# Later stores of split weights, a one-operation final norm for the last two expert pairs, and one branch around both overflow loops in a decoder block on one core

## The chip, the core and the metric

The kernel runs on one core of a Trainium2 chip. The metric is the device time of one execution in microseconds (us). The core has a matrix engine (TensorE, PE in the profile, with its weight loads PEld), a vector engine (VectorE, DVE), a scalar engine (ScalarE, ACT), a general engine (GpSimd, POOL) and SyncE (SP), which here only issues transfers. Each issues its instructions in order and waits for others by semaphores. A transfer (DMA) is issued by an engine's queue, and all transfers share 16 DMA engines. An instruction that waits in such a queue holds back what stands behind it.

## What is computed

The reference is one block of a hybrid decoder on 2048 tokens of width 1024, in float32. Cut to what matters here:

```
h = rmsnorm(x, norm1_g);  proj = h @ w_in            # q, k, v, r, a_low, u_pool and two gates
o = (head_rmsnorm(gla_mix(q, k, v, log_a)) * silu(r)) @ w_gla_branch
p = pool_mix(u_pool) @ w_pool_branch
x = x + (sigmoid(gate_gla) * o + sigmoid(gate_pool) * p) @ w_out
h2 = rmsnorm(x, norm2_g)
x = x + hier_moe(h2, ...)       # a group of 8 experts, 2 of them for each token, 32 in all
return rmsnorm(x, norm_f_g)
```

## The kernel before, in words

**Mixer.** Everything ahead of the experts is done in four blocks of 512 tokens (`block`, b = 0 to 3; the first ends near 250 us, the second near 575). A product is made in float16 with each operand split in a high half (hi) and what that leaves (lo). A 128 x 1024 piece of a weight is loaded as float32 by `stage` (L161). `halves` makes hi with an ACT operation (L177) and lo with a DVE operation (L178). Both lie in one buffer of the pool `wp`, which has 13 buffers (`NW`) for float32 pieces, split pieces and reloads alike. Since all blocks use the same weights, `halves` also stores the split piece to a DRAM tensor `wkeep` (L181), for some kinds of weight in block 0 and for the others in block 1 (`KEEP`); later blocks load it from there (`weight`, L170) and split nothing. In L161, L170 and L181, as in the transposing transfers of activations (L261 in `turn`, L686 in `turned`) and the loads of x (L275), the issuer is the queue of SP. So a store that waits for its lo half holds back what stands behind it there.

```
self.nc.sync.dma_start(f, self.A[mat][i])                                  # L161, in stage
nc.scalar.activation(w[:, 0, c:], f[:, c:], AF.Copy, scale=WSC)            # L177, in halves
nc.vector.scalar_tensor_tensor(w[:, 1, c:], f[:, c:], WSC, w[:, 0, c:], op0=OP.mult, op1=OP.subtract)
getattr(nc, self.KQ).dma_start(self.C[n][:, :, c:], w[:, :, c:])           # L181, KQ = 'sync'
```

A scheduler sets the order of the instructions on each engine in the mixer, working from the program's order and its own estimates; so a change in one place moves others. The matmuls of this part that are spoken of below: L339 (projections), L757 and L774 (the branches and the output product), L725 (folded weights), L522 (parts of the linear attention), L796 (the router's logits, which read the second norm's rows turned by the transfers of L261).

**Experts.** 16 pairs of experts follow (`moe`). For each, a plan of letters gives the order in which the steps are written: S splits weights, U and A are the up products and the activation, X, R and B fetch rows, D adds a product to a row tile and F (`finish`) applies the final norm to it and scatters it to the output. A pair has three row tiles: two of 128 rows x 1024 (i = 0, 1; PE line L1322, DVE line L1325) and one in which two halves of 64 rows stand side by side as 128 x 512 (i = 2; L1334, L1337). A row of a token that takes part in two pairs must only be normed the second time; the flags `l` and `nl` of a row say which. If a pair takes more rows than its tiles hold, `overflow` does the rest, and then no row is normed in `finish` but all at the end.

**The norm in `finish`.** `rstd` squares and sums a tile on ACT (L1365), joins the sums on DVE (L1367 to L1370) and takes the power on POOL (L1371). Then DVE multiplies by the flag (L1344), ACT makes a row factor gf * r + nl (L1346, or twice L1350 for halves of 64 rows) and DVE multiplies the tile by it (L1351). `scatter` (L1284) sends the rows from the queue of POOL. The g2 of the second norm has a copy, `g2q`, scaled by 32 (the root of 1024), which one form of the norm reads (`normed`, L232).

**The end.** `overflow` loads a count from memory on every engine (L1380), runs a loop so many times (L1382), loads a second count (L1438) and runs a second loop (L1439). With the inputs given both counts are zero. L1529 is the program's last line: what it shows is the end of the program on every engine.

Of the kernel before, what the change touches and what calls it, by code (L numbers as in the profile page):

```python
# [7 lines left out]
F32 = mybir.dt.float32  # L8
F16 = mybir.dt.float16
# [7 lines left out]
D = 1024  # L17
# [19 lines left out]
class Mixer:  # L37
# [10 lines left out]
    def pools(self):  # L48
# [14 lines left out]

        self.C, self.kept = tc.dram_tile([16 + 40 + 24, 128, 2, 1024], F16, name="wkeep"), {}
# [24 lines left out]
    def consts2(self):  # L89
# [22 lines left out]
        self.g2q = self.cx.tile([128, D], F32, name="g2q")  # L112
        V.tensor_scalar(self.g2q, self.g2, float(D) ** 0.5, None, op0=OP.mult)
# [45 lines left out]
    def stage(self, mat, i):  # L159
        f = self.wp.tile([128, 1024], F32, name="w", bufs=self.NW)  # L160
        self.nc.sync.dma_start(f, self.A[mat][i])  # L161
        return f

    def weight(self, mat, i, f=None, c=0):
# [5 lines left out]
        nc.sync.dma_start(w[:, :, c:], self.C[self.kept[mat, i]][:, :, c:])  # L170
        return w

    def halves(self, f, key, c=0):
# [42 lines left out]
    def normed(self, x, g, store=None, quick=False, new=None):  # L216

        nc = self.nc
        if quick:
# [11 lines left out]
            for y, n in zip(ys, q):  # L231
                nc.vector.scalar_tensor_tensor(y, x[:, n], r[:, 0:1], self.g2q[:, n], op0=OP.mult, op1=OP.mult)  # L232
# [569 lines left out]
    def block(self, b, tail):  # L802

        last = b + 1 == self.NB
        self.blk = b
        self.hT, self.L7, self.L7c = self.hTn, self.sevens(self.Hn, self.HSn), self.sevens_c(self.Hn, self.HSn)
# [56 lines left out]
        if last:  # L863
            self.xo = {t: self.x_load(b, t) for t in range(TT)}
# [206 lines left out]
    def spill(self):  # L1071
# [31 lines left out]
        V.tensor_scalar(none[:, 0:1], none[:, 0:1], 0.5, None, op0=OP.is_lt)  # L1103
        for _, _, l, _ in self.tab:
# [26 lines left out]
    def moe(self):  # L1131
# [18 lines left out]
        with tc.manual_schedule(engines={getattr(E, e) for e in self.MANUAL}) if self.MANUAL else ExitStack():  # L1150
            for P in range(self.NP + 1):
                for c in (self.PLAN if P else self.PLAN.replace("U0 A0 U1 A1", "V0 V1 W0 A0 W1 A1")).split():
# [186 lines left out]
    def finish(self, s, i):  # L1339

        nc = self.nc
        x, o, _, l, nl = s["X"][i]
        y, r = self.rstd(x)
# [7 lines left out]
        nc.vector.tensor_tensor(y, x, y, op=OP.mult)  # L1351
        t = self.scatter(y, o).ins
# [21 lines left out]
    def overflow(self):  # L1374
# [7 lines left out]
        with tc.For_i(0, n):  # L1382
            T = lambda name, sh, dt=F32: mp.tile([128] + sh, dt, name="o" + name)
            le = T("le", [32])
            V.tensor_scalar(le, self.ct, self.it, None, op0=OP.is_le)
            e = T("e", [1])
            V.tensor_reduce(e, le, axis=AX.X, op=OP.add)
            ei = T("ei", [1], I32)
            V.tensor_copy(ei, e)
            V.tensor_scalar(le, self.i32, e, None, op0=OP.is_equal)  # L1390
            st = T("st", [32])
            V.tensor_tensor(st, self.ct, self.nt, op=OP.subtract)
            V.tensor_tensor(st, st, le, op=OP.mult)
            base = T("base", [1])
            V.tensor_reduce(base, st, axis=AX.X, op=OP.add)
            V.tensor_tensor(base, self.it, base, op=OP.subtract)
            V.tensor_tensor(st, self.capE, le, op=OP.mult)
            cap = T("capt", [1])
            V.tensor_reduce(cap, st, axis=AX.X, op=OP.add)
            V.scalar_tensor_tensor(base, base, 128.0, cap, op0=OP.mult, op1=OP.add)  # L1400
            rel, oth = T("rel", [nt * 2]), T("oth", [nt * 2])
            V.tensor_scalar(oth, self.ex.rearrange("p t k -> p (t k)"), e, OOB, op0=OP.not_equal, op1=OP.mult)
            V.tensor_scalar(rel, self.rk.rearrange("p t k -> p (t k)"), base, None, op0=OP.subtract)
            V.tensor_tensor(rel, rel, oth, op=OP.add)
            io = T("io", [128])
# [127 lines left out]
```

## Time and profile before

| | us |
|---|---|
| runs: 1673.47, 1674.84, 1676.40; median | 1674.84 |
| the profiled execution's own time | 1676.06 |
| its span, first to last instruction | 1674.3 |
| PE busy | 1530.3 (91%) |
| DVE busy | 1074.3 (64%) |
| ACT busy | 686.0 (41%) |
| POOL busy | 607.7 (36%) |
| mean granted clock of PE | 0.96 of full speed |

The profile is one execution. Its time is 1.8 us above its span and 1.2 us above the median of the runs. Busy times are shares of the whole span; where the engine that sets the pace changes from stage to stage, the tables by stretch tell more than these.

### The profile page before, as it was taken

Reading aid. Unit: us, or ns where it says so; the run is one execution under the profiler, and the core shown is the slowest. Engines: PE = TensorE matmul, PEld = TensorE weight load, DVE = VectorE, ACT = ScalarE, POOL = GpSimd, SP = SyncE. Lnnn points to the kernel's source line nnn. Section 1 sums busy time; section 2 is a strip of 40 time slices with the busy share of each in tenths; the row PEclk is TensorE's granted clock in tenths of the full one; section 3 lists DMA queues with packets and bytes.
Section 4 is the critical chain, followed back from the end, with each engine's and each line's share of the span. In section 5 each row is a group of like instructions: output and inputs, shape, how many; then the busy total and the mean of one; then the engine's idle time right before and its main releaser. Section 6 shows DMA issues by size and latency. Waiting matters only on the chain.

```text
span 1674.3 us, 27694 instructions
## 1 busy us (share of the span) xinstructions
PE 1530.3 (91%) x10587; PEld 914.6 (55%) x10587; DVE 1074.3 (64%) x1898; ACT 686.0 (41%) x1056; POOL 607.7 (36%) x543
## 2 busy tenths in 40 slices
PE   5898978987999898999989999996799999999994
PEld 3364333435744343764434674443668787777773
DVE  8669685589954543772624674337577777777762
ACT  5623453453223352122423021113356665666661
POOL 1356382356523401342322241121343444444431
PEclk9999999989999999999989999998799999999997
DMA  7434659797775989565878756759599999999941
GB/s 267 133 117 141 232 189 249 230 293 234 231 259 164 250 287 286 182 194 179 231 192 246 245 160 201 204 159 315 187 313 332 336 328 341 333 325 326 330 164 43
DMA packets 244808, 394.65 MB, mean 236 GB/s; under 512 B 154507, under 2 KB 157963, under 8 KB 244672
## 3 DMA queue, kind: packets, MB, share of 16 engines
q1 hardware_dynamic: 222144, 324.50, 62.5%
q0 software_dynamic: 22528, 68.35, 11.5%
q8 instruction: 84, 1.38, 0.3%
q14 instruction: 52, 0.43, 0.1%
HBM read 294.03 MB, written 75.50 MB: 221 GB/s over the span
## 4 chain that ended last, share of the span: by engine, by line
PE 66%; DVE 11%; DMA 7%; issue 6%; POOL 4%; SPq 3%; ACT 2%; POOLq 0%; DVEq 0%; ACTq 0%
PE acc L1297 14%; PE aux L339 8%; PE acc L774 8%; PE acc L339 8%; PE acc L1322 7%; PE acc L522 6%; PE acc L757 6%; DMA w<-in_wv_dram 4%; PE acc L1334 3%; DVE w L178 3%; DMA bt<-bt 2%; SPq L261 2%; PE auxh L1241 2%; PE acc L591 1%; POOL w L398 1%
## 5 line engine op out<-in xcount | busy, mean ns | idle before, releaser
L1297 PE MATMUL acc<-xT,mwh 128*128 128x184 f16 (+2 forms) x3264 | 249.8, 239 | 0.0
L1297 PEld LDWEIGHTS <-mwh 128*128 128x128 f16 x3264 | 244.6, 98 | 7.6 <-issue 7.6
L178 DVE SCALAR_TENSOR_TENSOR w<-w 128x1024 f16<-128x1024 f32 x106 | 144.2, 1369 | 88.5 <-ACT w L177 88.2
L774 PE MATMUL acc<-w,bt 128*128 128x512 f16 x768 | 174.4, 389 | 16.1 <-DMA bt<-bt 12.9
L339 PEld LDWEIGHTS <-hS 128*128 128x128 f16 x1056 | 104.5, 100 | 133.4 <-issue 18.0
L757 PE MATMUL acc<-w,bt 128*128 128x512 f16 x768 | 169.0, 381 | 7.1 <-ACT w L177 7.1
L177 ACT ACTIVATE w<-w 128x1024 f16<-128x1024 f32 x106 | 108.0, 1028 | 151.8 <-DMA w<-in_wv_dram 75.2
L1203 DVE SCALAR_TENSOR_TENSOR mwh<-mst,mwh 128x1024 f16<-128x1024 f32 x128 | 153.4, 1219 | 23.6 <-ACT mwh L1202 23.4
L1202 ACT ACTIVATE mwh<-mst 128x1024 f16<-128x1024 f32 x128 | 128.7, 1049 | 60.7 <-PE acc L1297 59.8
L774 PEld LDWEIGHTS <-bt 128*128 128x128 f16 x768 | 76.0, 100 | 113.2 <-issue 14.5
L339 PE MATMUL aux<-w,hS 128*128 128x512 f16 x528 | 131.6, 398 | 4.5 <-DVE w L178 2.5
L339 PEld LDWEIGHTS <-hT 128*128 128x128 f16 x792 | 77.2, 98 | 100.9 <-issue 11.1
L522 PEld LDWEIGHTS <-w 128*128 128x128 f16 x1176 | 114.3, 100 | 32.4 <-issue 10.5
L757 PEld LDWEIGHTS <-bt 128*128 128x128 f16 x768 | 75.3, 98 | 99.9 <-issue 10.9
L339 PE MATMUL acc<-w,hS 128*128 128x512 f16 x528 | 123.1, 382 | 0.0
L1322 PE MATMUL acc<-msd,sg 128*128 128x512 f32 x256 | 115.7, 605 | 0.0
L762 POOL TENSOR_TENSOR et<-et 128x512 f32<-128x512 f32 x32 | 40.5, 1269 | 174.9 <-DVE et L760 174.9
L684 ACT ACTIVATE bt<-et 128x512 f16<-128x512 f32 x48 | 30.2, 628 | 174.4 <-POOL et L762 100.6
L348 DVE SCALAR_TENSOR_TENSOR et<-aux,et 128x512 f32<-128x512 f32 x99 | 65.8, 683 | 53.5 <-PE aux L339 53.5
L339 PE MATMUL aux<-w,hT 128*128 128x512 f16 x396 | 91.8, 379 | 5.7 <-DVE w L178 3.3
L760 DVE SCALAR_TENSOR_TENSOR et<-acc,et 128x512 f32<-128x512 f32 x64 | 43.3, 689 | 82.4 <-PE acc L757 82.4
L339 PE MATMUL acc<-w,hT 128*128 128x512 f16 x396 | 92.3, 379 | 0.9 <-DVE w L178 0.9
(293 smaller groups left out, 2493.8 us busy)
## 6 DMA issues: line engine op xcount, KB each, us to landing
w<-wkeep SPq DMA_DIRECT2D x172, 512.0 KB, 4.7
mst<-in_we_dram SPq DMA_DIRECT2D x128, 512.0 KB, 6.0
wkeep<-w SPq DMA_DIRECT2D x70, 512.0 KB, 3.3
msd<-in_we_dram SPq DMA_DIRECT2D x64, 512.0 KB, 7.1
w<-in_wv_dram SPq DMA_DIRECT2D x60, 512.0 KB, 4.9
x<-in_x_dram SPq DMA_DIRECT2D x32, 512.0 KB, 5.5
w<-in_wm_dram SPq DMA_DIRECT2D x16, 512.0 KB, 6.1
out_dram<-x POOLq DMA_DIRECT2D x16, 512.0 KB, 5.8
```

The source lines that it names most:

```text
L177: nc.scalar.activation(w[:, 0, c:], f[:, c:], AF.Copy, scale=WSC)
L178: nc.vector.scalar_tensor_tensor(w[:, 1, c:], f[:, c:], WSC, w[:, 0, c:], op0=OP.mult, op1=OP.subtract)
L339: nc.tensor.matmul(p, L[name](i, c, k), w[k // 2][:, a, (k % 2) * 512:(k % 2 + 1) * 512], start=k == 0 and m == 0, stop=k == 3 and m == 2)
L348: nc.vector.scalar_tensor_tensor(o[i], ps[i], DSC, x[i], op0=OP.mult, op1=OP.add)
L522: nc.tensor.matmul(ps[:, :h], w[:, i, k * 128:(k + 1) * 128], L[name](c, k), start=k == 0 and m == 0, stop=k == 3 and m == 2)
L757: nc.tensor.matmul(ps, lhs, w[k // 2][:, a, (k % 2) * 512:(k % 2 + 1) * 512], start=k == 0 and i == 0, stop=k == 3 and i == 2)
L774: nc.tensor.matmul(ps, self.mT[t][k // 4][:, 4 * c + k % 4], w[hf][k // 2][:, a, (k % 2) * 512:(k % 2 + 1) * 512], start=k == 0 and i == 0 ...
L1202: nc.scalar.activation(w[:, 0], f, AF.Copy, scale=WSC)
L1203: nc.vector.scalar_tensor_tensor(w[:, 1], f, WSC, w[:, 0], op0=OP.mult, op1=OP.subtract)
L1297: nc.tensor.matmul(ps[:, c * CAP + lo:c * CAP + hi], self.part(W[o], col, 128, a), xT[:, b, k, lo:hi], start=k == 0 and i == 0, stop=k == ...
L1322: nc.tensor.matmul(ps, s["ac"][i][:, f, :128], self.part(s["W"][3 * i + 2], f * D + hf * 512, 512), start=f == 0, stop=f == 1)
L1334: nc.tensor.matmul(ps[hf * 64:(hf + 1) * 64], s["ac"][h][:, f, CAP - 64:], self.part(s["W"][3 * h + 2], f * D + hf * 512, 512), start=q == ...
```

## The change

1. `halves` no longer issues its store. It appends it to a list, `self.stores`, with the number of weight loads issued so far. After each weight load (`stage` or a reload in `weight`) `loaded` issues those stores that are two or more loads old, each with a note to the scheduler that it comes after that load. A list that is not empty is emptied at the start of each block (`flush`).
2. `g2q` is gone. In the last block `g2` is scaled in place, and the norm reads it.
3. Ahead of the experts, `spill` makes a flag `ln`, two small factors `lq` and a copy `gl` of gf for the case that no tile overflowed, with three small DVE operations and one ACT operation.
4. `finish` of pairs 14 and 15 no longer looks at a row's flags. For a 128 x 1024 tile ACT squares two halves into two sums; DVE adds them with the norm's epsilon, POOL takes the power, DVE adjusts it, and one DVE operation multiplies the tile by the row's factor and `gl`. A 64-row tile takes the old `rstd` and two such operations.
5. In the last pair the plan has the 64-row tile first: D2 F2 D0 F0 D1 F1 in place of D0 F0 D1 F1 D2 F2.
6. Both loops of `overflow` stand within one branch on the first count.

```diff
-        self.nc.sync.dma_start(f, self.A[mat][i])
+        self.loaded(self.nc.sync.dma_start(f, self.A[mat][i]).ins)
         return f
+    AHEAD = 2
+    def loaded(self, ins):
+        self.nload += 1
+        while self.stores and self.stores[0][0] + self.AHEAD <= self.nload:
+            with self.tc.issue_after(ins):
+                self.store1()
+    def store1(self):
+        _, n, w, c = self.stores.pop(0)
+        getattr(self.nc, self.KQ).dma_start(self.C[n][:, :, c:], w[:, :, c:])
...
-            getattr(nc, self.KQ).dma_start(self.C[n][:, :, c:], w[:, :, c:])
+            self.stores.append((self.nload, n, w, c))
...
-        V.tensor_scalar(self.g2q, self.g2, float(D) ** 0.5, None, op0=OP.mult)
...
+        V.tensor_copy(self.ln, none[:, 0:1])
+        V.tensor_scalar(self.lq[:, 0:1], none[:, 0:1], float(D) ** 0.5, None, op0=OP.mult)
+        V.tensor_scalar(self.lq[:, 1:2], none[:, 0:1], -1.0, 1.0, op0=OP.mult, op1=OP.add)
+        nc.scalar.activation(self.gl, self.gf, AF.Identity, bias=self.lq[:, 1:2], scale=self.ln[:, 0:1])
...
+                if P == self.NP - 1:
+                    plan = plan.replace("D0 F0 D1 F1 D2 F2", "D2 F2 D0 F0 D1 F1")
...
+                for h in range(2):
+                    c = slice(h * 512, h * 512 + 512)
+                    nc.scalar.activation(y[:, c], x[:, c], AF.Square, accum_out=ss[:, h:h + 1])
+                nc.vector.tensor_scalar(r, ss[:, 0:1], ss[:, 1:2], D * EPS, op0=OP.add, op1=OP.add)
+                nc.gpsimd.tensor_tensor(r, r, self.mhalf[:, 0:1], op=OP.pow)
+                nc.vector.tensor_scalar(r, r, self.lq[:, 0:1], self.lq[:, 1:2], op0=OP.mult, op1=OP.add)
+                nc.vector.scalar_tensor_tensor(y, x, r, self.gl, op0=OP.mult, op1=OP.mult)
...
-        with tc.For_i(0, n):
+        with tc.If(n > 0):
+            with tc.For_i(0, n):
```

The change moves instructions in the whole mixer. Three places matter below. In the rows a number behind a name tells buffers apart; numbers and lines differ between the two programs for the same step (L161 and L160 load a weight, L181 and L174 store a split one, L261 and L277 turn rows, L275 and L291 load x).

**The queue of SP in block 1, where rows are turned for the first logits** (bt_2649 and bt_2650 before, bt_2647 and bt_2648 now). Before:

```order
L161 DMA w_2831<-in_wv_dram 128x1024
L181 DMA wkeep_79<-w_2793 128x2048
L181 DMA wkeep_79<-w_2797 128x2048
L161 DMA w_2833<-in_wv_dram 128x1024
L275 DMA x_4541<-in_x_dram 128x1024
L181 DMA wkeep_79<-w_2837 128x2048
L181 DMA wkeep_79<-w_2841 128x2048
L181 DMA wkeep_79<-w_2906 128x2048
L261 DMA_TRANSPOSE bt_2649<-bt_2575 128x8x128
L261 DMA_TRANSPOSE bt_2650<-bt_2576 128x8x128
```

The same place in the changed program:

```order
L160 DMA w_2827<-in_wv_dram 128x1024
L291 DMA x_4539<-in_x_dram 128x1024
L160 DMA w_2829<-in_wv_dram 128x1024
L174 DMA wkeep_79<-w_2791 128x2048
L174 DMA wkeep_79<-w_2794 128x2048
L277 DMA_TRANSPOSE bt_2647<-bt_2573 128x8x128
L277 DMA_TRANSPOSE bt_2648<-bt_2574 128x8x128
L291 DMA x_4584<-in_x_dram 128x1024
L160 DMA w_3040<-in_wv_dram 128x1024
L160 DMA w_3042<-in_wv_dram 128x1024
L174 DMA wkeep_79<-w_2835 128x2048
L174 DMA wkeep_79<-w_2838 128x2048
```

Three stores (w_2837, w_2841, w_2906) that stood ahead of the two transposes stand behind them, and the load of x stands ahead of the last weight load.

**The queue of SP between block 0 and block 1, where the rows of block 1 are turned** (hT, hS) and weights of block 0's output product are loaded. Before:

```order
L261 DMA_TRANSPOSE hT_2114<-et_2187 128x8x128
L161 DMA w_2249<-in_wv_dram 128x1024
L261 DMA_TRANSPOSE hS_2115<-et_2208 128x8x128
L261 DMA_TRANSPOSE hS_2115<-et_2209 128x8x128
L261 DMA_TRANSPOSE hS_2115<-et_2212 128x8x128
L261 DMA_TRANSPOSE hS_2115<-et_2213 128x8x128
L161 DMA w_2369<-in_wv_dram 128x1024
L275 DMA x_2389<-in_x_dram 128x1024
L275 DMA x_2417<-in_x_dram 128x1024
```

Now:

```order
L277 DMA_TRANSPOSE hT_2108<-et_2183 128x8x128
L277 DMA_TRANSPOSE hS_2109<-et_2204 128x8x128
L160 DMA w_2245<-in_wv_dram 128x1024
L174 DMA wkeep_79<-w_2140 128x2048
L174 DMA wkeep_79<-w_2143 128x2048
L277 DMA_TRANSPOSE hS_2109<-et_2205 128x8x128
L277 DMA_TRANSPOSE hS_2109<-et_2208 128x8x128
L277 DMA_TRANSPOSE hS_2109<-et_2209 128x8x128
L291 DMA x_2387<-in_x_dram 128x1024
L291 DMA x_2415<-in_x_dram 128x1024
L160 DMA w_2367<-in_wv_dram 128x1024
```

The load of w_2249 (now w_2245) has one transpose more ahead of it, and that of w_2369 (now w_2367) two stores and two loads of x more.

**DVE at the end of the last pair** (mx_ tiles are the three row tiles, y the normed rows). Before:

```order
L1337 SCALAR_TENSOR_TENSOR mx_10479<-acc,twr,mx_10479 128x512
L1344 TENSOR_TENSOR frs<-frs,tlm 128x1
L1367 COPY frs<-fss 64x1
L1368 COPY frs<-fss 64x1
L1369 TENSOR_TENSOR fss<-fss,frs 128x1
L1370 TENSOR_SCALAR frs<-fss 128x1
L1351 TENSOR_TENSOR y<-mx_10478,y 128x1024
L1344 TENSOR_TENSOR frs<-frs,tlr 128x1
L1351 TENSOR_TENSOR y<-mx_10479,y 128x512
```

Now:

```order
L1356 SCALAR_TENSOR_TENSOR mx_10477<-acc,twm,mx_10477 128x512
L1394 SCALAR_TENSOR_TENSOR y<-mx_10478,frs,gl 64x512 x2
L1387 TENSOR_SCALAR frs<-frs,slq 128x1
L1385 TENSOR_SCALAR frs<-fs_17137 128x1
L1388 SCALAR_TENSOR_TENSOR y<-mx_10476,frs,gl 128x1024
L1387 TENSOR_SCALAR frs<-frs,slq 128x1
L1388 SCALAR_TENSOR_TENSOR y<-mx_10477,frs,gl 128x1024
```

The operation after the last product (L1337 before, L1356 now) is followed by one that finishes the 64-row tile, and the last operation makes a whole 128-row tile.

## Rows read from the trace of the kernel before

**Rows 1.** The page: share of the chain that ended last, by engine.

```profile
PE 66%; DVE 11%; DMA 7%; issue 6%; POOL 4%; SPq 3%; ACT 2%; POOLq 0%; DVEq 0%; ACTq 0%
```

**Rows 2.** Stretches of 20 us: busy PE, PEld, DVE, ACT, POOL; granted clock; DMA.

```profile
260.00:280.00 20.00, 13.64 (x57) 5.80 (x56) 8.71 (x10) 4.01 (x5) 5.99 (x4) 0.83 1.03 238
...
340.00:360.00 20.00, 15.86 (x88) 7.03 (x87) 18.88 (x20) 13.22 (x19) 10.81 (x9) 0.89 0.90 271
360.00:380.00 20.00, 15.61 (x75) 6.25 (x73) 16.12 (x19) 7.27 (x8) 8.16 (x8) 0.76 1.10 311
...
400.00:420.00 20.00, 13.25 (x104) 10.65 (x104) 20.00 (x45) 4.26 (x7) 13.51 (x10) 0.93 0.49 172
...
sum 340.00, PE 291.98 PEld 154.52 DVE 264.72 ACT 143.81 POOL 179.00; mean PE 17.18 PEld 9.09 DVE 15.57 ACT 8.46 POOL 10.53
```

**Rows 3.** Waits of SP's queue, whole span: total us, times, longest.

```profile
SPq L181 <- DVE w L178: 115.2, 39, 9.2
```

**Rows 4.** Waits of PE, 100 to 430 us: total, times, longest.

```profile
PE aux L796 <- DMA bt<-bt: 7.9, 3, 3.7
PE acc L757 <- ACT w L177: 7.1, 2, 6.4
...
PE aux L725 <- DMA w<-in_wv_dram: 4.5, 2, 3.0
```

**Rows 5.** Waits of SP's queue, 340 to 360 us.

```profile
SPq L181 <- DVE rms L211: 5.4, 1, 5.4
```

**Rows 6.** PE in order of time, 345 to 375 us: start, us, what, idle before.

```profile
344.75 7.07 PE L339 MATMUL acc<-w,hS 128*128 128x512 f16 x32
354.29 0.19 PE L796 MATMUL aux<-wrh,bt 128*128 128x36 f16 x1 [2.47 <-DMA bt<-bt]
...
357.29 4.43 PE L339 MATMUL aux<-w,hS 128*128 128x512 f16 x10
...
370.69 0.21 PE L796 MATMUL aux<-wrh,bt 128*128 128x36 f16 x1 [3.73 <-DMA bt<-bt]
```

**Rows 7.** ACT in order of time, 255 to 300 us.

```profile
280.15 1.06 ACT L177 ACTIVATE w<-w 128x1024 f16<-128x1024 f32 x1 [5.89 <-DMA w<-in_wv_dram]
286.83 1.06 ACT L177 ACTIVATE w<-w 128x1024 f16<-128x1024 f32 x1 [5.62 <-DMA w<-in_wv_dram]
```

**Rows 8.** PE in order of time, 235 to 300 us.

```profile
274.32 6.77 PE L757 MATMUL acc<-w,bt 128*128 128x512 f16 x24 [6.36 <-ACT w L177]
```

**Rows 9.** DVE in order of time, 10 to 40 us.

```profile
20.43 0.69 DVE L113 TENSOR_SCALAR g2q<-g2r 128x1024 f32<-128x1024 f32 x1
```

**Rows 10.** The stretch of the experts, in the columns of rows 2.

```profile
1240.00:1640.00 400.00, 400.00 (x3793) 304.46 (x3791) 295.47 (x481) 249.09 (x330) 164.56 (x162) 1.00 0.88 308
```

**Rows 11.** ACT in order of time, 1185 to 1215 us.

```profile
1203.06 2.00 ACT L1202 ACTIVATE mwh<-mst 128x1024 f16<-128x1024 f32 x2 [13.14 <-PE acc L1297]
```

**Rows 12.** The chain that ended last, in order of time: start, us, what.

```profile
1649.32 3.61 PE acc L1334 x16
```

**Rows 13.** DVE and POOL in order of time, from 1651 us.

```profile
1652.95 0.75 DVE L1337 SCALAR_TENSOR_TENSOR mx<-acc,twr,mx 128x512 f32<-128x512 f32 x1 [0.99 <-PE acc L1334]
...
1655.03 0.15 DVE L1370 TENSOR_SCALAR frs<-fss 128x1 f32<-128x1 f32 x1
1655.66 1.23 DVE L1351 TENSOR_TENSOR y<-mx,y 128x1024 f32<-128x1024 f32 x1 [0.48 <-ACT y L1346]
...
1658.72 0.69 DVE L1351 TENSOR_TENSOR y<-mx,y 128x512 f32<-128x512 f32 x1 [1.76 <-ACTq L1382]
...
1659.68 0.99 POOL L1284 DMA_INDIRECT out_dram<-y,tih  x1 [1.48 <-DVE y L1351]
```

**Rows 14.** Lines L1382, L1439, L1529: ns min/median/max, first and last start.

```profile
L1382 POOLq INC_SWDGE_SEM  x1: 1832/1832/1832, 1661.2 to 1661.2; - x1
...
L1439 POOLq COMPARE_BRANCH  x3: 33/33/39, 1665.2 to 1666.5; - x3
...
L1529 POOLq DRAIN  x3: 40/109/6772, 1666.7 to 1674.0; - x3
```

More of the change, by code (lines that the diff above doesn't have):

```diff
@@ L62, in pools @@
         self.H = tc.dram_tile([self.NTOK, 2, D], F16, name="h2d")
+        self.stores, self.nload = [], 0
         self.C, self.kept = tc.dram_tile([16 + 40 + 24, 128, 2, 1024], F16, name="wkeep"), {}
@@ L160, in stage, with flush @@
         f = self.wp.tile([128, 1024], F32, name="w", bufs=self.NW)
-        self.nc.sync.dma_start(f, self.A[mat][i])
+        self.loaded(self.nc.sync.dma_start(f, self.A[mat][i]).ins)
         return f
+    AHEAD = 2
[7 more added lines that the diff above has]
+        getattr(self.nc, self.KQ).dma_start(self.C[n][:, :, c:], w[:, :, c:])
+    def flush(self):
+        while self.stores:
+            self.store1()
     def weight(self, mat, i, f=None, c=0):
@@ L231, in normed @@
             for y, n in zip(ys, q):
-                nc.vector.scalar_tensor_tensor(y, x[:, n], r[:, 0:1], self.g2q[:, n], op0=OP.mult, op1=OP.mult)
+                nc.vector.scalar_tensor_tensor(y, x[:, n], r[:, 0:1], g[:, n], op0=OP.mult, op1=OP.mult)
             hi = [nc.scalar.activation(hh[0][:, n], y, AF.Copy).ins for y, n in zip(ys, q)]
@@ L863, in block @@
         if last:
+            nc = self.nc
+            nc.vector.tensor_scalar(self.g2, self.g2, float(D) ** 0.5, None, op0=OP.mult)
             self.xo = {t: self.x_load(b, t) for t in range(TT)}
@@ L1151, in moe @@
             for P in range(self.NP + 1):
-                for c in (self.PLAN if P else self.PLAN.replace("U0 A0 U1 A1", "V0 V1 W0 A0 W1 A1")).split():
+                plan = self.PLAN
+                if P == 0:
+                    plan = plan.replace("U0 A0 U1 A1", "V0 V1 W0 A0 W1 A1")
+                if P == self.NP - 1:
+                    plan = plan.replace("D0 F0 D1 F1 D2 F2", "D2 F2 D0 F0 D1 F1")
+                for c in plan.split():
                     f, d = {"U": (self.mo_up, 0), "V": (lambda s, h: self.mo_up(s, h, 0, 128), 0),
@@ L1339, in finish @@
     def finish(self, s, i):
-        nc = self.nc
+        nc, mp = self.nc, self.mp
         x, o, _, l, nl = s["X"][i]
+        if s["P"] >= 14:
+            n = x.shape[1]
+            if n == D:
+                ss = mp.tile([128, 2], F32, name="fs2", bufs=2)
+                r = mp.tile([128, 1], F32, name="frs", bufs=3)
+                y = mp.tile([128, D], F32, name="y", bufs=3)
+                for h in range(2):
[5 more added lines that the diff above has]
+                nc.vector.scalar_tensor_tensor(y, x, r, self.gl, op0=OP.mult, op1=OP.mult)
+            else:
+                y, r = self.rstd(x)
+                nc.vector.tensor_scalar(r, r, self.ln[:, 0:1], self.lq[:, 1:2], op0=OP.mult, op1=OP.add)
+                for h in range(2):
+                    p = slice(h * 64, h * 64 + 64)
+                    nc.vector.scalar_tensor_tensor(y[p], x[p], r[p], self.gl[p, h * 512:(h + 1) * 512], op0=OP.mult, op1=OP.mult)
+            return self.put(s, i, y, o)
         y, r = self.rstd(x)
@@ L1351, in finish, with put @@
         nc.vector.tensor_tensor(y, x, y, op=OP.mult)
+        self.put(s, i, y, o)
+    def put(self, s, i, y, o):
         t = self.scatter(y, o).ins
```

132 lines of the change are left out of this document (67 added, 65 removed).

## The prediction

> **What bounds the kernel now.** I began with the chain that ended last. PE holds 66% of it, then come DVE with 11%, transfers with 7% and the queue of SP with 3% [rows 1]. So PE is the pace, and a gain has to come from where PE stands idle. The table by stretches says where that is. From 1240 to 1640 us PE is busy 400.00 of 400.00 us [rows 10]: in the experts nothing done beside PE can pay. From 100 to 440 us PE is busy 291.98 of 340 us, so 48.0 us are idle [rows 2]. These are block 0 and the first half of block 1, where the weights are split and stored. After the last matmul there is a tail without PE.
>
> Of the 48 us I read who was waited for. Three waits of the logits (L796) for turned rows cost 7.9 us, two of L757 for a hi half 7.1 us, two of L725 for a weight load 4.5 us [rows 4]. In SP's queue the stores (L181) wait 115.2 us in 39 waits for DVE's lo halves [rows 3], and whatever stands behind a waiting store waits too. That is the thing the change attacks. But DVE is itself busy 18.88 of 20 us at 340 to 360 and 20.00 of 20 us at 400 to 420 [rows 2]: there, work that arrives earlier still has to go through DVE.
>
> **The change, part by part.** All of it is a sum of us against the profiled execution; minus is a gain.
>
> *Stores, logits of block 1: -4.* The first logits matmul starts at 354.29 after 2.47 us of waiting for its turned rows, the third wait is 3.73 us [rows 6], and so the second is 7.9 - 2.47 - 3.73 = 1.7 us. In the old order three stores stand ahead of the transposes; one of these waits 5.4 us [rows 5]. In the new order the three stand behind. The two transposes can then go some 5 us or more earlier, which covers the first two waits (4.2 us). The third stays, since five stores stand ahead of its transposes now. Idling also lowers the clock: 32 matmuls took 7.07 us (221 ns each) ahead of the waits, 10 took 4.43 us (443 ns each) behind [rows 6], the two levels 2.4 and 1.2 GHz. The granted clock was 0.89 and 0.76 in the stretches from 340 to 380, worth (0.11 + 0.24) x 20 = 7.0 us of full speed [rows 2], half of it, 3.5 us, behind the first two waits. So at most 4.2 + 3.5 = 7.7 us are to be had. What holds against it is DVE: from 340 to 380 it is idle only 1.1 + 3.9 = 5.0 us, and from 400 on not at all [rows 2], so PE cannot come out further ahead than that. Between 0 and 7.7 I take 4.
>
> *Stores, everywhere else: -1.* The waits of L757 and L725 sum to 11.6 us [rows 4]. The order moves some of their loads ahead of a store, but most of the loads that are late have ten transposes ahead, or stand where DVE is full. Bounds: 0 and -11.6. I take -1, near the DVE row.
>
> *Two loads that come later: +1.5.* Between blocks 0 and 1 the chain is load, hi half, matmul: L757 waits 6.36 us for a hi half [rows 8], and the hi halves at 280.15 and 286.83 follow waits of 5.89 and 5.62 us for their loads [rows 7]. In the new order one of these loads has one transpose more ahead of it, the other two stores and two x loads more, with the transfers busy all the time (share 1.03 at 260 to 280 [rows 2]). PE had no slack there: 274.32 + 6.77 = 281.1 [rows 8] is about where the next hi half was ready. A transpose is bounded by the 2.47 us that PE waited for one pair [rows 6]. Bounds: 0, if the loads were waiting for buffers anyway, and +9.8, a second wait such as the 6.36 us with its clock loss (0.17 x 20 = 3.4 us [rows 2]). I take 1.5, between half a pair of transposes and a whole one.
>
> *g2q: -0.6.* One operation of 0.69 us [rows 9] leaves the start, where DVE works back to back; scaling g2 in the last block costs the same where DVE has room. Bounds -0.7 and 0.
>
> *gl, lq, ln, pair 14: 0.* `gl` is one ACT operation on a tile of 128 x 1024, an estimated 1.2 us by DVE's 1.23 us for that shape [rows 13]; it falls into 13.14 us in which ACT is idle [rows 11]. Pair 14's `finish` runs beside a PE that is 100% busy [rows 10]. If that cover were gone, this would be some 1.2 us more.
>
> *Tail of pair 15: -1.3.* Before, the last matmul ends at 1649.32 + 3.61 = 1652.93 [rows 12] and the last scatter begins at 1659.68 [rows 13], 6.75 us later: product added on DVE, square on ACT, power on POOL, row factor on ACT, product on DVE, one after the other and twice. Now DVE's queue sets the end. Behind the last matmul it does L1356 (0.75, as L1337), two 64-row products (2 x 0.69), three small ones (3 x 0.15) and two of 128 rows (2 x 1.23) [rows 13]: 0.75 + 1.38 + 0.45 + 2.46 = 5.04 us. The chain through ACT and POOL for the last tile runs beside that and is shorter. With some 0.4 us for semaphores the last scatter begins at 5.4, so 1.3 us are gained. That scatter has 128 rows instead of 64 halves, and lands later, but behind it stand 13 us in which nothing waits for it but SP. Bounds -0.5 and -1.7.
>
> *The branch: -3.5.* After the last scatter comes an increment on POOL, 1661.2 + 1.83 = 1663.0; then the second count and the second loop's branches until 1666.5; then a DRAIN on POOL of 6.77 us from 1666.7, and the span ends at 1674.3 [rows 14]. With the branch only the increment stays, so DRAIN can begin at about 1663.2: 1666.7 - 1663.2 = 3.5 us earlier. Bounds: -3.7, all between, and 0. Here a rule speaks against: in the second loop's three branches on POOL, 33 to 39 ns each within 1.3 us [rows 14], I see no stall. The Trainium skill (Runtime: NRT & Kernel Launch, Instruction fetch mechanics) says that a taken branch to a target outside the instructions already fetched waits for them to be fetched. The new branch jumps over both bodies and has no hint ahead of it in the order. By that rule the term would shrink towards 0; by the rows it is -3.5.
>
> Sum: -4 - 1 + 1.5 - 0.6 - 1.3 - 3.5 = **-8.9 us**. From the profiled execution's 1676.06 that gives 1667.2; that execution was 1.2 us above the median of the runs, 1674.84, and from there it gives 1665.9. I forecast **1666.0 us**.
>
> **Rivals.**
>
> *A. DVE binds the mixer, and the stores change nothing there.* For: the 20.00 of 20 us [rows 2]. Against: the logits' waits are for transposes, not for DVE [rows 4]. Then only -0.6, -1.3, -3.5 and +1.5 stay: 1674.84 - 3.9 = 1670.9. The Trainium skill (Perfetto Trace Analysis, Identifying the Most-Contended Engine) says to work first on the engine with the highest occupancy; by that rule moving stores in a queue, with DVE's work as it was, would give this time.
>
> *B. The branch gives nothing,* because DRAIN lasts the longer, waiting for something that ends when it did, or the jump costs what it saves. For: only one DRAIN is seen, and its 6.77 us are not explained [rows 14]. Then 1665.9 + 3.5 = 1669.4.
>
> *C. Slower: a weight load that PE needs comes so late between blocks 0 and 1 that PE stalls once more as at 268 us.* Place and price: 6.36 us [rows 8] and 3.4 us of clock, 9.8 in all, with no gain from the stores. 1674.84 - 5.4 + 9.8 = 1679.2. For: the two x loads now ahead, and the full transfers (1.03 [rows 2]). It decides once the loss is over 5.4 + 3.35 = 8.75 us.
>
> *D. The change doesn't do what it says:* two loads later is often still ahead of the lo half, and the store waits in the queue all the same, with others behind it. Then the mixer keeps its time and the end gains 4.8: 1670.0. For: the third transposes still have stores ahead. Against: the old waits are up to 9.2 us [rows 3], about what two loads take.
>
> **How the numbers follow.** Chances: forecast 0.54, A 0.16, B 0.10, C 0.12, D 0.08. A measurement of this kernel tells about 0.2% from no change, 3.35 us, so "faster" is under 1671.5 and "slower" over 1678.2. The forecast, with terms between their bounds, gives 0.50 of faster and 0.04 of same; A at 1670.9 lies near the line, 0.09 and 0.06 and 0.01 of slower; B 0.08 and 0.02; D 0.06 and 0.02; C 0.10 of slower and 0.02 of same. Sums: 0.73, 0.16, 0.11. The range reaches up past A, B and D to 1675, and leaves out C. Down it takes 7.7 for the logits, 4 for the rest, no late load, and the end's bounds: 1674.84 - 7.7 - 4 - 0.7 - 1.7 - 3.7 = 1657.0.
>
> **What would show it.** Right: the first two logits of block 1 start with no wait, the granted clock from 350 to 365 us is 1.00, SP's stores wait far less than 115 us; the last scatter begins some 5.4 us after the last matmul; POOL's DRAIN begins within 0.5 us of the increment's end and lasts 6.8 us. Wrong: PE's idle time from 100 to 440 us still near 48 us, with DVE in place of transfers as what it waits for (A); a longer DRAIN (B); a new wait of PE for a hi half at 270 to 300 us with half clock behind it (C); long waits of the store line in SP's queue with loads behind them (D).

## The result, and the profile after

The changed kernel takes 1699.07 us (median of 4 runs, 1696.45 to 1702.27) beside 1675.62 for the kernel before; the ratio is 1.0144 with a 95% interval of 1.0121 to 1.0168, so it is **slower by some 24 us**, clear of the noise. I had forecast 1666.0, faster. The profiled execution took 1701.07 us with a span of 1699.3, 25.0 more than the span of before.

To find where the time went I took the nth matmul of PE in either trace and subtracted its start before from its start after. Both have 10587 of them; where their order differs, the difference is only roughly that of one piece of work. (How far two executions in the same order drift apart is told in the last section.) It is 2.8 us at 149 us, 5.2 at 282, 12.4 at 297, 13.4 at 388 and 20.7 from 451 us on, all in the stretch where weights are split and stored. It is 22.7 from about 670 us to the end of the mixer, 26.6 in the experts, and the last matmul ends 27.1 us later (1680.02 against 1652.93). The end gives 2.1 us back, so the span is 25.0 longer.

The windows view of the changed kernel, in the columns of rows 2, shows the stretch; its last row ends at the matmul that stands at 469.3 us in the kernel before:

```profile
100.00:440.00 340.00, 284.29 (x1528) 146.85 (x1527) 248.39 (x335) 142.27 (x211) 177.32 (x110) 0.93 0.70 212
100.00:490.00 390.00, 328.15 (x1843) 179.24 (x1842) 291.12 (x429) 154.48 (x250) 201.62 (x130) 0.93 0.70 212
```

In 340 us PE did less than before (284.29 us busy against 291.98 [rows 2]). The same view of the kernel before, up to the same matmul:

```profile
100.00:469.30 369.30, 321.28 (x1844) 176.03 (x1843) 291.13 (x428) 151.61 (x248) 195.22 (x129) 0.95 0.72 224
```

So for the same matmuls PE needs 20.7 us more: idle time went from 369.3 - 321.28 = 48.0 to 390 - 328.15 = 61.9 us (13.9 more), and busy time rose by 6.9 us, at a granted clock of 0.93 in place of 0.95. DVE's busy time is the same to the hundredth (291.12 and 291.13 us).

What PE waits for, 100 to 440 us of the changed kernel (five of the rows; total us, times, longest):

```profile
PE acc L773 <- ACT w L193: 9.0, 3, 3.7
PE aux L355 <- DVE w L194: 7.4, 4, 2.5
PE acc L790 <- ACT w L193: 6.1, 1, 6.1
PE aux L1002 <- DVE rt32b L999: 4.0, 1, 4.0
PE aux L812 <- DMA bt<-bt: 3.9, 3, 2.1
```

The logits (L812, before L796) do wait less, 3.9 us for 7.9 [rows 4]. Up to the same matmul, all waits for transfers fell from 12.4 to 8.3 us. In their place, those for hi halves (L193) rose from 11.9 to 20.1, and the routing (L1002 and, behind 440 us, L1059), for which PE did not wait before, costs 10.0; those for lo halves (L194) rose from 11.6 to 13.4. What SP's queue waits for, 100 to 480 us, in the changed kernel:

```profile
SPq L174 <- DVE w L194: 58.3, 18, 9.1
SPq L702 <- POOL bt L701: 43.0, 9, 16.5
```

and the row of the stores before, in the same stretch (115.2 in the whole span [rows 3]):

```profile
SPq L181 <- DVE w L178: 93.5, 31, 9.2
```

Summed over all releasers, the stores' waits fell from 171.3 to 84.2 us, those of the transposes rose from 52.9 to 97.7, of the weight loads (L160) from 18.6 to 51.6. The sum over the queue is 257.0 before and 254.7 after. **The queue waits as long as it did; only what it waits in front of has changed.** A queue that either issues or waits can hardly do otherwise in a stretch of fixed length, so this sum alone doesn't show that a shorter wait of the stores is worth nothing. But the queue didn't get through more either: it issued 166 transfers in these 380 us, before 175.

### The profile page after: what moved, and what is told of

Same layout as the page of the kernel before. It is cut to its first block, busy times and chain, and to the rows that moved or that the text cites. A ratio compares the mean times of both kernels' runs of the same rounds, so it can differ in the third digit from the quotient of the medians.

```text
span 1699.3 us, 27530 instructions
## 1 busy us (share of the span) xinstructions
PE 1539.2 (91%) x10587; PEld 917.6 (54%) x10587; DVE 1078.4 (63%) x1903; ACT 682.1 (40%) x1057; POOL 614.8 (36%) x543
## 5 line engine op out<-in xcount | busy, mean ns | idle before, releaser
L194 DVE SCALAR_TENSOR_TENSOR w<-w 128x1024 f16<-128x1024 f32 x106 | 147.2, 1399 | 103.9 <-ACT w L193 103.8
L193 ACT ACTIVATE w<-w 128x1024 f16<-128x1024 f32 x106 | 107.6, 1028 | 154.6 <-DMA w<-in_wv_dram 72.4
```

## The experiments

In the first batch I split the change in parts, with one theory being that the postponed stores cost all of it, and two ways for that: they spoil the order of the work, or the buffers of the weights come free later, so that one buffer more gives the time back.

**e1_stores_at_once**: the change, but each store is issued at once.

```diff
-            self.stores.append((self.nload, n, w, c))
+            getattr(nc, self.KQ).dma_start(self.C[n][:, :, c:], w[:, :, c:])
```

> The changed kernel, with each store issued where it was before (in halves, at once); all other parts of the change stay. Theory H (held buffers): a store that waits for two more loads keeps its buffer of the 13 in use, later weight loads wait for a buffer, PE starves; then nearly all of the mixer's loss is gone, PE's idle time from 100 to 440 us is again near 48 us, and the time is about 1675.6 - 3.2 (branch) + 1.1 (longer end of the last pair) = 1673.5 us, give or take 3. Theory S (reshuffle): any edit makes the scheduler order blocks 0 and 1 anew, by 10 us and more either way, and the stores are not special; then the time lies anywhere from 1665 to 1700 and the mixer differs from before by several us even without the postponed stores. Theory R (the other parts, g2q and gl among them, cost the time): it stays near 1699.

Measured: 1668.28 us, ratio 0.998 (0.9964 to 0.9996), that is -3.3 us. From 451 to 570 us its matmuls stand 0.3 us ahead of those of before, where the change's stood 20.7 us behind.

**e2_stores_only**: the kernel before with `stores`, `loaded`, `store1` and `flush` alone, as in the diff above.

> The kernel before, with the postponed stores as its only edit (list, two loads, emptied at the start of a block). Theory H: the mixer loses some 20 us as in the changed kernel, the end is unchanged: about 1698 us, SP's loads wait 40 us or more for buffers between 100 and 480 us (47 us in the changed kernel, 11 us before). Theory S: a time that differs from the sum of parts by several us, as the scheduler orders it differently again. Theory R: about 1675.

Measured: 1696.02 us, ratio 1.0162 (1.0136 to 1.0187), +27 us. With e1 this closes the sum: 1.0162 x 0.998 = 1.0142, against 1.0144 for the whole. The stores are the whole loss; all else gains 3.3 us.

**e3_branch_only**: the kernel before with `with tc.If(n > 0):` around the two loops.

> The kernel before, with the one branch around both overflow loops as its only edit. From the changed kernel's trace the stretch from the last scatter's start to the end of the span fell from 14.6 to 11.5 us, so 3.2 us less: 1672.4 us if the order of the mixer stays as it was (the edit lies behind it, so it should). Rival: the saving is a matter of where the last scatter lands, then less than 1 us.

Measured: 1667.46 us, ratio 0.9984 (0.997 to 0.9997), that is -2.7 us. From the end of the last matmul to the end of the span it takes 18.2 us, before 21.4: -3.2, by one profile each.

**e4_14_buffers**: the change with one weight buffer more.

```diff
-    NW, NET, NBT = 13, 19, 13
+    NW, NET, NBT = 14, 19, 13
```

> The changed kernel with 14 buffers in place of 13 in the pool of weights (the room of g2q). Theory H: one more buffer gives back part of the loss, 5 us or more: below 1694 us, and SP's loads wait less for buffers. Theory S: another order, so a change of either sign. Theory R: no change within 3 us of 1699.

Measured: 1693.64 us, ratio 1.0144 (1.0116 to 1.0172), the change's own ratio. The time lies just under the 1694 us of the theory, but only because the kernel before took 1670.3 us beside it and not 1675.6; by the ratio, nothing came back. A shortage of buffers, as I had put it, finds no support here. Since the scheduler was free to order this kernel anew as well, e11 is the cleaner test.

A store that is issued at another place does two things. It changes SP's queue, and the scheduler that orders all engines then comes to another order for the others too. The next batch parts these. A table read from one kernel's built order is laid over another's instructions, up to the end of block 1, by dependencies without semaphores:

```diff
             tail = m.block(b, tail)
+            if b == 1:
+                pin(tc)   # for each engine: instruction k+1 of the table after instruction k
```

If the cost sits in SP's queue, it goes with the late stores; if in the order of the computing engines, it goes with the order. By the traces the pin does what it should and adds nothing: PE, DVE, ACT and POOL have as many operations as before, and in e5 (and e13, below) those of the first 440 us stand in the order of before without exception. SP's queue is not pinned in e5 and e6; of its 134 loads and transposes in that stretch, leaving out the stores, one stands elsewhere in e5 and three in e6.

**e5_late_stores_old_order**: e2, with PE, DVE, ACT and POOL in the order of before.

> The postponed stores as the only edit of the kernel before, but PE, DVE, ACT and POOL are held to the very order in which the kernel before has their instructions up to the end of block 1; only the queue of SP has another order. Theory Q (queue): the loss lies in SP's queue, where late stores come in bunches ahead of loads and transposes; then the time is still near 1.016 times that of before (some +25 us). Theory S2 (order): the loss lies in the other order that the scheduler gives to the computing engines once the stores are late; then it is within 5 us of before, or a little faster, since the queue is freer.

Measured: 1679.69 us, ratio 1.005 (1.0033 to 1.0067), +8.4 us.

**e6_old_stores_late_order**: the kernel before, stores at once, with the four engines in e2's order.

> The mirror of the run with the old order: stores at once as before, but PE, DVE, ACT and POOL are held to the order that they have in the kernel with the postponed stores alone, up to the end of block 1. Theory Q: within 5 us of before. Theory S2: near +25 us, as with postponed stores. Both at once: something between, and the two runs tell the shares.

Measured: 1689.25 us, ratio 1.0114 (1.0098 to 1.0129), +19 us. The two make up e2: 1.005 x 1.0114 = 1.0165. **Some 70% of the loss is the order of the computing engines, 30% the queue.** By the two traces, counted over the first 440 us of the kernel before, 333 of 2001 places on PE, 207 of 467 on DVE, 127 of 298 on ACT and 40 of 153 on POOL hold another instruction in e6. Up to the matmul that stands at 469.3 us before, e6 takes this (columns of rows 2):

```profile
98.49:483.58 385.09, 329.77 (x1844) 179.54 (x1842) 289.69 (x429) 154.41 (x250) 199.65 (x130) 0.93 0.71 216
```

That is 15.8 us more than the 369.3 of before: PE is idle for 55.3 us in place of 48.0, and busy for 8.5 us more at a lower granted clock (0.93 for 0.95). Its waits for hi halves rose from 11.9 to 16.4 us and those for lo halves from 11.6 to 16.1, while those for transfers fell from 12.4 to 5.1.

**e7_old_plan_order**: e1 without the new order of pair 15.

```diff
-                if P == self.NP - 1:
-                    plan = plan.replace("D0 F0 D1 F1 D2 F2", "D2 F2 D0 F0 D1 F1")
```

> The changed kernel with stores at once and the last pair in the old order D0 F0 D1 F1 D2 F2. Its fellow with the order D2 F2 D0 F0 D1 F1 starts the last scatter 7.8 us after the last matmul, the kernel before 6.8. With the 64-row tile last: product added 0.75, square 0.63 and its sum 0.19, four small DVE operations 0.6, power 0.54, small 0.15, two products of 0.69: 4.2 us and some 0.8 for semaphores, so 5.0, and no scatter of the tile stands ahead of a power on POOL. 2.8 us less than with the new order: about 1665.5 where the other took 1668.3 and before 1670.3. Rival: the two scatters of the 128-row tiles hold POOL and the power waits for them as before; then 1668.

Measured: 1667.22 us, ratio 0.9969 (0.9955 to 0.9983), -5.2 us: faster than both kernels. Its interval overlaps e1's, so that it beats e1 isn't shown by the times. From the end of the last matmul (1645.33 + 3.65 = 1648.98) to the last scatter it takes 6.6 us, not the 5.0 that I expected: of the 2.8 us that were to come off e1's 7.85, some 1.3 came. The rest isn't accounted for.

**e8_one_load_ahead**: e2 with `AHEAD = 1`.

> The kernel before with stores postponed by one load in place of two. Theory Q: the loss grows with the delay, so about half of it, +12 us. Theory S2: any postponement gives the scheduler another order, and the loss needs not be half; anything from 0 to +25 us.

Measured: 1684.42 us, ratio 1.0079 (1.0062 to 1.0097), +13 us: half of e2's loss, as either theory allows.

In the third batch I asked which engine's order costs, and what the queue's part is.

**e9_pe_old_rest_late**: as e6, but PE in the order of before; DVE, ACT and POOL in e2's.

> Stores at once; DVE, ACT and POOL held to the order of the kernel with postponed stores, PE to the order of the kernel before, up to the end of block 1. All four engines in the late order cost 1.14%, about 19 us. Theory V: the loss lies in the order of the engines that prepare PE's operands (lo halves stand up to 12 operations earlier in DVE's queue in block 1 and what PE needs behind them); then it stays at 1.0% or more. Theory P: the loss lies in PE's own order (its logits and attention matmuls stand elsewhere); then it is under 0.3%.

Measured: 1695.09 us, ratio 1.0133 (1.0103 to 1.0163), +22 us. The interval overlaps that of e6. PE's own order is not what costs; the order of the engines that feed it is. Which of the three it is, no run tells.

**e10_one_ahead_old_order**: e5 with `AHEAD = 1`.

> Stores postponed by one load, with PE, DVE, ACT and POOL held to the order of the kernel before. With two loads this cost 0.5%, 8.4 us, in SP's queue alone. If the loss in the queue grows with the delay, 0.25% or so; if the delay itself does not matter, 0.5% again; if a short delay helps, below 0.

Measured: 1682.19 us, ratio 1.0068 (1.0047 to 1.0089): no less than with two loads. The queue's part doesn't grow with the delay; what e8 saved was in the order of the engines.

**e11_14_buffers_old_order**: e5 with 14 weight buffers. The room for it comes from `g2q`, which is left out as in the change.

> Stores postponed by two loads, PE, DVE, ACT and POOL held to the order of the kernel before, and 14 buffers of weights in place of 13 (g2q gone to make room). Theory H in its small form: the 0.5% that the queue costs is waiting of loads for buffers that late stores hold; then 14 buffers give it back, 0.0 to 0.2%. Theory B (bunches: late stores go out in threes and fours and take queue and transfers from loads and transposes): the 0.5% stays.

Measured: 1680.98 us, ratio 1.0056 (1.0039 to 1.0072): a buffer more doesn't help here either.

**e12_scatter_behind_power**: e1, with the 64-row tile's scatter put behind the last power on POOL.

```diff
-                nc.gpsimd.tensor_tensor(r, r, self.mhalf[:, 0:1], op=OP.pow)
+                pw = nc.gpsimd.tensor_tensor(r, r, self.mhalf[:, 0:1], op=OP.pow).ins
+                if s["P"] == 15 and i == 1:
+                    with self.tc.issue_after(pw):
+                        self.put(*self.held)
```

> The changed kernel with stores at once, and the scatter of the last pair's 64-row tile put behind the power of the last 128-row tile in POOL's queue, where it stood ahead. In the run with stores at once, POOL spends 1.76 us on that scatter while the last power waits, and DVE's last product waits 1.6 us for the power; the last scatter starts 7.85 us after the last matmul. If that is what made the end long, it now starts 6.2 us after the last matmul; if DVE sets the end, as forecast, nothing changes.

One execution, so by its trace alone: 1666.33 us. The last matmul ends at 1645.78, the last scatter begins at 1652.91, 7.13 us later, in e1 7.85. So 0.7 of the 1.65 us that I expected; the rest became a new wait:

```profile
1648.57 1.53 POOL L1386 TENSOR_TENSOR frs<-frs,mhalf 128x1 f32<-128x1 f32 x1 [2.36 <-DVE frs L1385]
1650.28 1.04 POOL L1315 DMA_INDIRECT out_dram<-y,tih  x1 [0.18 <-issue]
1651.62 0.98 POOL L1315 DMA_INDIRECT out_dram<-y,tim  x1 [0.30 <-issue]
1652.91 0.98 POOL L1315 DMA_INDIRECT out_dram<-y,tim  x1 [0.30 <-DMA out_dram<-y,tih]
```

In these rows (POOL in order of time) the power takes 1.53 us, and then three scatters stand one behind the other, 1.3 us apart.

e5 still left open whether late stores cost by themselves (theory L), or the order of SP's loads and transposes, which the scheduler had rebuilt around them (theory R).

**e13_stores_alone_late**: the kernel before with all five engines' queues pinned to its own order, and only the stores moved in SP's queue, each behind the second load after it.

> Before, with every engine and SP's loads, transposes and x loads pinned to before's order up to the end of block 1; only the 88 stores are moved in SP's queue, each behind the second load after it. Theory L (a store that is issued later costs by itself: the buffer of its weights comes free later and its bytes collide with a load): ratio near 1.005, as with late stores in the old order of the engines. Theory R (the half per cent came with the other order of SP's loads and transposes that the scheduler made, not with the stores): ratio within 0.998 to 1.002. The prediction's own idea (the late stores free the queue) would show here, if anywhere, as a ratio of 0.997 or less.

Measured: 1680.29 us, ratio 1.005 (1.0032 to 1.0069). Theory R falls: **late stores alone, with not one instruction of another engine moved up to the end of block 1, cost half a per cent.** (Behind that the scheduler is free; the first matmul that stands elsewhere comes at about 650 us.) Waits of SP's queue in e13, 100 to 480 us:

```profile
SPq L686 <- POOL bt L685: 45.2, 9, 17.3
SPq L161 <- DMA wkeep<-w: 18.7, 7, 6.3
SPq L181 <- DVE w L178: 16.9, 10, 4.2
```

The stores' wait for lo halves is down to 16.9 us (93.5 before), and the kernel is slower for it. Loads (L161) now wait 18.7 us for a late store to land, since it holds the buffer that they take (yet by e11 one buffer more gives nothing back), and 16.1 us for lo halves; the turned operands of L686 wait 45.2 (26.3 before). The waits of the whole queue sum to 257.2 us, before to 257.0. The same at one place, SP in order of time, e13 (the first row, for the first two logits, and then those for the third):

```profile
342.96 5.98 SPq L261 DMA_TRANSPOSE bt<-bt  x2
357.87 0.49 SPq L161 DMA_DIRECT2D w<-in_wv_dram  x1
358.41 0.90 SPq L181 DMA_DIRECT2D wkeep<-w  x2
359.40 0.52 SPq L161 DMA_DIRECT2D w<-in_wv_dram  x1
359.97 3.94 SPq L181 DMA_DIRECT2D wkeep<-w  x5
364.85 10.67 SPq L261 DMA_TRANSPOSE bt<-bt  x2
```

and the kernel before:

```profile
348.48 4.39 SPq L261 DMA_TRANSPOSE bt<-bt  x2
355.77 0.32 SPq L181 DMA_DIRECT2D wkeep<-w  x1
356.19 1.40 SPq L161 DMA_DIRECT2D w<-in_wv_dram  x2
357.68 1.10 SPq L181 DMA_DIRECT2D wkeep<-w  x1
358.83 8.18 SPq L261 DMA_TRANSPOSE bt<-bt  x2
```

Stores that wait one by one for their lo halves become a bunch of five ahead of the transposes, whose turned rows the third logits need. These transposes begin 6.0 us later than before, and the third logits (at 370.7 us before) are 6.0 us late.

Ahead of that, what the prediction expected did happen in e13. The transposes of the first two logits begin 5.5 us earlier, these logits do not wait (2.47 and 1.67 us before), and the granted clock from 345 to 365 us is 1.00 (0.83 before):

```profile
345.00:365.00 20.00, 17.74 (x103) 8.18 (x102) 18.59 (x21) 13.35 (x20) 9.92 (x9) 1.00 0.75 214
```

PE, 4.5 us behind the kernel before at 316 us, is 2.6 us ahead of it at 363. Then it waits for a hi half, a lo half and the third logits' turned rows, 10.3 us where it had waited 3.7 [rows 6]:

```profile
365.61 0.59 PE L339 MATMUL acc<-w,hT 128*128 128x512 f16 x2 [2.52 <-ACT w L177]
369.44 2.72 PE L339 MATMUL acc<-w,hT 128*128 128x512 f16 x6 [3.24 <-DVE w L178]
376.67 0.21 PE L796 MATMUL aux<-wrh,bt 128*128 128x36 f16 x1 [4.51 <-DMA bt<-bt]
```

e5 shows the same: the first two logits do not wait, the clock from 345 to 365 us is 1.00, and the lead is gone by the third.

## Why the prediction was wrong

**The step that failed is "Stores, logits of block 1: -4" together with "everywhere else: -1".** The sum has no term for the other engines' order, which it took as given (+19 us, e6), and it took a store that waits in SP's queue for time lost (-5 forecast, +8.4 measured with the order held, e5). Both were wrong.

*The order (+19 us of 27, e6).* I looked at the built order only in the places that the prediction spoke of. One place shows how an order costs: DVE from the first reduction of the routing to the operand that PE's matmul L1002 needs. The changed kernel (DVE, of the rows between only the lo halves):

```profile
402.73 0.17 DVE L973 TENSOR_REDUCE rt<-L 128x4 f32<-128x16 f32 x1
408.38 2.28 DVE L194 SCALAR_TENSOR_TENSOR w<-w 128x1024 f16<-128x1024 f32 x1
416.52 1.98 DVE L194 SCALAR_TENSOR_TENSOR w<-w 128x1024 f16<-128x1024 f32 x1
420.03 1.81 DVE L194 SCALAR_TENSOR_TENSOR w<-w 128x1024 f16<-128x1024 f32 x2
426.18 2.26 DVE L194 SCALAR_TENSOR_TENSOR w<-w 128x1024 f16<-128x1024 f32 x1
428.36 1.34 DVE L999 TENSOR_TENSOR rt32b<-rt,rt 128x128 bf16<-128x128 f32 x1
```

then the PE row that waits for it, and two rows of POOL:

```profile
429.76 0.27 PE L1002 MATMUL aux<-rt32b,tri 128*128 128x128 bf16 x1 [4.03 <-DVE rt32b L999]
408.30 1.28 POOL L581 TENSOR_TENSOR w<-w 128x512 f32<-128x512 f32 x1
409.54 2.25 POOL L582 TENSOR_TENSOR w<-w 128x512 f32<-128x512 f32 x1
```

and the kernel before (DVE, chosen in the same way):

```profile
391.83 0.15 DVE L954 TENSOR_REDUCE rt<-L 128x4 f32<-128x16 f32 x1
398.90 1.22 DVE L178 SCALAR_TENSOR_TENSOR w<-w 128x1024 f16<-128x1024 f32 x1
403.62 1.21 DVE L178 SCALAR_TENSOR_TENSOR w<-w 128x1024 f16<-128x1024 f32 x1
406.33 1.19 DVE L178 SCALAR_TENSOR_TENSOR w<-w 128x1024 f16<-128x1024 f32 x1
408.37 1.35 DVE L980 TENSOR_TENSOR rt32b<-rt,rt 128x128 bf16<-128x128 f32 x1
```

The chain takes 428.36 - 402.73 = 25.6 us, before 16.5, so 9.1 more. Five whole lo halves, 8.3 us, stand among it; before it was three and a half, 4.3 us (the half one, of 0.68 us, is not shown). That is 4.0 of the 9.1, and not all of it for their number: three of the five take 1.98 to 2.28 us, where those of before take 1.19 to 1.22. The one at 408.38 starts beside a POOL product (408.30 to 409.58) and ends 1.1 us after it; the next POOL product then takes 2.25 us in place of some 1.3. The same 26 operations of the routing account for 4.2 us more (several of them take 1.0 to 1.35 us here and 0.2 to 0.3 there, one the other way round), and two more of other work for the rest. So what an order costs depends on what DVE and POOL do at the same time, too. PE waits 4.0 us, where it had not waited at all. I had read DVE as full there (20.00 of 20 us [rows 2]) and taken that as a reason for a smaller gain, not for a loss. This row is a part of the whole change's loss, not a measured part of the 19 us: in e6 PE waits only 0.2 us at it, and the 19 us lie in many waits of 1 to 4 us and in the lower clock behind them.

*The queue (+8.4, e5 and e13).* The prediction counted 115.2 us of stores waiting [rows 3], "and whatever stands behind a waiting store waits too". The queue's wait from 100 to 480 us is 250 to 261 us in every kernel here but e8 (269), with stores early or late: SP mostly waits for work that isn't ready, and what a store no longer waits, the transpose or load behind it does. At e13's place a store that waits is also what had kept the stores from bunching in front of a transpose. The step was right for the first two logits, as e13 shows, and stopped one step too early: the sum didn't ask what the third logits, and the hi and lo halves ahead of them, would then wait for.

*Two loads that come later, +1.5.* The place was right, and the size wrong. Between 281.7 and 296.7 us the loss rises from 5.2 to 12.4. The hi half there is late for its load (ACT), and PE waits for it:

```profile
288.64 1.06 ACT L193 ACTIVATE w<-w 128x1024 f16<-128x1024 f32 x1 [7.75 <-DMA w<-in_wv_dram]
300.12 1.06 ACT L193 ACTIVATE w<-w 128x1024 f16<-128x1024 f32 x1 [4.88 <-DMA w<-in_wv_dram]
```

```profile
301.23 11.84 PE L790 MATMUL acc<-w,bt 128*128 128x512 f16 x42 [6.14 <-ACT w L193]
```

This is rival C, 6.36 and 3.4 us [rows 2, 8] foretold and 7.2 found. C was the only rival with the right sign, but it took this one stall for the whole, 1679.2; the others of the kind were not counted. How sure the 7.2 is, is another matter: in e2, with the same late stores, the loss between the same two matmuls goes from 8.0 to 8.5 only. With the order held, e13 has a stall of this kind (4.44 us at 293 us), and e5 none that is longer than one of before (1.0 and 1.6 us, where before has 2.55 at 297).

*Logits.* Their waits fell by 4.0 us (7.9 to 3.9), which is the forecast's number by luck: the first two were to lose all of their 4.1 us and lost 1.6 (0.47 and 2.10 us are left), and the third, which was to keep its 3.73, fell to 1.37. The granted clock from 350 to 365 us is 0.89, not 1.00. And nothing came of it: the first logits begin 4.5 us later than before (358.76 for 354.29), the third 11.6 us later (382.30 for 370.69).

*Rivals A, B and D.* A (1670.9) and D (1670.0) leave the mixer's time as it was; they fall by e2, where the stores alone cost 27 us. B falls by e3: the branch is worth about what was forecast (-2.7, -5.0 to -0.5, by the runs; -3.2 by the traces).

*g2q, gl, lq, ln and pair 14.* -0.6 and 0. No run takes them alone. e1 as a whole gives -3.3 (-6.0 to -0.7), where the terms without stores summed to -5.4.

*Tail of pair 15: -1.3.* Measured +1.1: from the last matmul's end to the last scatter it takes 7.83 us, before 6.75. POOL and DVE at the end of the changed kernel:

```profile
1683.08 1.76 POOL L1315 DMA_INDIRECT out_dram<-y,tih  x1 [2.64 <-ACTq L1438]
1684.87 0.58 POOL L1386 TENSOR_TENSOR frs<-frs,mhalf 128x1 f32<-128x1 f32 x1
```

```profile
1682.64 1.28 DVE L1388 SCALAR_TENSOR_TENSOR y<-mx,frs,gl 128x1024 f32<-128x1024 f32 x1
1685.48 0.27 DVE L1387 TENSOR_SCALAR frs<-frs,slq 128x1 f32<-128x1 f32 x1 [1.56 <-POOL frs L1386]
1685.79 1.28 DVE L1388 SCALAR_TENSOR_TENSOR y<-mx,frs,gl 128x1024 f32<-128x1024 f32 x1
```

```profile
1687.85 0.98 POOL L1315 DMA_INDIRECT out_dram<-y,tim  x1 [1.19 <-DVE y L1388]
```

I had written that DVE's queue sets the end and that "the chain through ACT and POOL for the last tile runs beside that and is shorter". It isn't: the last power stands in POOL's queue behind a scatter of 1.76 us that itself waits for its rows, and DVE waits 1.56 us for the power. The products cost 1.28 and 1.50 us, near the forecast's 1.23 and 2 x 0.69. From the end of the last product (1687.07) to the scatter 0.78 us pass, where before it was 0.27 [rows 13]; the forecast had 0.4 for all semaphores together. Why this grew is open.

*The branch: -3.5.* Measured -3.2, in the traces of the change and of e3. From the start of the last scatter to the end of the span it takes 1699.3 - 1687.85 = 11.45 us, before 1674.3 - 1659.68 = 14.6. The closing lines of POOL's queue (columns as in rows 14):

```profile
L1438 POOLq INC_SWDGE_SEM  x1: 1814/1814/1814, 1689.8 to 1689.8; - x1
```

```profile
L1586 POOLq DRAIN  x3: 44/113/6770, 1691.7 to 1699.0; - x3
```

DRAIN begins within 0.1 us of the increment's end and lasts 6.77 us as before [rows 14]. By the rows the jump costs nothing that shows. Of the stall that the Trainium skill names for a taken branch (Runtime: NRT & Kernel Launch, Instruction fetch mechanics) no trace here shows a sign.

What stays open: which of DVE, ACT and POOL carries the 19 us, and why the scheduler's order is the worse one. That the 19 us come with the order is shown; the chain above is one place of it, not the proof of a cause.

## What to carry to other kernels

A queue's wait in front of a store is worth something only if the work behind that store is ready by then: sum the waits of the whole queue, and ask what is late next, before counting it as a gain. Where a scheduler orders the engines, a moved DMA can reorder them all; compare the whole order of every engine, above all of one that is full, and pin the order to tell the two effects apart. On an engine that issues DMAs in order at the end of a kernel, put what the last result needs ahead of every scatter that can wait (0.7 us in e12, in one execution).

## What was not expected of the hardware

A POOL operation that starts while DVE does a 128 x 1024 product takes longer. The scatter at 1683.08 starts inside the product of 1682.64 to 1683.92 and takes 1.76 us; the two behind it take 1.03 and 0.98. In e12 the power at 1648.57 takes 1.53 us in place of 0.58, inside a product that began at 1648.40 and took 1.28. The Trainium skill (SBUF — State Buffer, SBUF: two separate sides) says that such a DVE operation with two inputs from SBUF holds the ports that it shares with GpSimd against a GpSimd operation that reads SBUF, and that whichever of the two starts first blocks the other until it ends. The rows agree: both POOL operations end 0.4 to 0.9 us after the product does, and so no sooner than it. So do the lo half at 408.38 and the POOL products beside it, shown above, where POOL was first. But a scatter that is first holds up nothing that shows: that at 1685.63 starts 0.16 us ahead of the last product, which takes 1.28 us like the one before.

Two executions whose instructions have the same order up to the end of the mixer differ: e3's matmuls lie up to 4.0 us behind those of before (at 367 us) and from 670 us on up to 3.2 ahead of them. So a difference of two single profiles below some 4 us says nothing by itself, and a step of up to 7 us inside one comparison can be chance; the shares above rest on the ratios of the runs.
